# A trunk layer on one core: order of residual loads, of bank copies against weight casts, and start of the token sums

## The chip, the cores and the metric

The kernel runs on one core of one Trainium2 chip. The metric is the time of one execution in device microseconds (us); smaller is better. Times of before are the median of three runs; a run of the profiler adds one more execution whose instructions are known one by one.

## What is computed

One layer of a decoder, for 512 tokens and 1024 channels, all in float32. Cut to its steps:

```python
u = rmsnorm(h, norm1_g)
a_glu, q, k, v, r, g_low, gate_a, gate_b = split_cols(u @ w_in)
c = a_glu[..., :1024] * sigmoid(a_glu[..., 1024:])
y_conv = silu(layernorm(causal_dwconv(c, 31))) @ w_conv_out
y_gla = gated_linear_attention(q, k, v, g_low, r) @ w_gla_out
h = h + (sigmoid(gate_a) * y_conv + sigmoid(gate_b) * y_gla) @ w_o
u2 = rmsnorm(h, norm2_g)
z = causal_dwconv(u2 @ w_ffn_up, 3)                 # 2 x 2816 channels
h = h + (silu(z[..., :2816]) * z[..., 2816:]) @ w_ffn_down
return rmsnorm(h, final_g)
```

## The kernel before, in words

**Products.** A float32 operand is held as two parts, `hi` (its value rounded to float32r, the type in which TensorE takes it) and `lo` (what is left). One product of two operands is three matmuls (`mm3`, L363 to L365). A weight tile of 128x1024 is loaded into a buffer `raw` (four of them) by SP's queue, cast by ScalarE to `whi` (L295, L312), and its `wlo` is either subtracted by VectorE (L296, L321) or, for tiles in `ADDED`, made by a negating ScalarE copy (L314) and an accumulating load from GpSimd's queue (L315). `split_weight` does one tile, `prefetch(n)` as many as are missing until n tiles lie ready ahead of those used, and `weight` takes the next one, with `prefetch` around it. The order of all tiles is one list, `order`; asking for a tile out of this list's order isn't possible.

**Seven products for eight.** Some projections split rows and columns in halves and form a 2x2 block product with seven products instead of eight (`seven` for `w_o` and `w_down`, `unit` for `w_r`, `up_seven` for seven of the 22 pairs of the up projection, those in `UP_SEVEN`: 6, 7, 10, 11, 14, 15, 18). The steps are called a11, a12, s1, n2, n3, s4 and a22; sums of operands go into some of them. `up_seven(i)` uses four weights: b and x (two column tiles as loaded, x becoming a sum of both), n, and m (a half tile, cast at L288 and subtracted at L289 into a `raw` buffer). The sums of weights are `up_operand` (L257): two additions on VectorE, two on GpSimd, when x is asked for. While TensorE runs the steps, it also runs parts of another tile's product (`beside`) between them.

**Banks in `up_seven`.** One bank, `x` here (a PSUM bank, `ax` in the profile), takes a11, then n2 is added to it, then n3. In between ScalarE copies it out: after a11 into `n0` (L1456), after n2 negated into `n1` (L1462), after n3 into `n0` (L1466). The next step that writes to the bank has to wait for the copy. Bank `y` (s1) is copied into `att` at L1459. VectorE then makes two sums (L1468, L1469), and the convolution of width 3 (L1266 on ScalarE, L1268 on VectorE), Silu (L1274), the product of both halves (L1276) and the parts for the down projection (L1281 ScalarE's cast, L1282 and L1289 to L1301 VectorE) follow.

**Output projection.** `seven("w_o", ...)` adds its products into the residual, eight tiles `hres[t, n]` of 128x512, token tile t and column half n (L1188). The tiles are loaded from x at L1221, all from SP's queue, just ahead of it. Step a11 and a12 add to [0, 0] and [1, 0], s1 to [2, 1] and [3, 1], n2 and s4 to [0, 1] and [1, 1], n3 to [2, 1] and [3, 1], a22 to [2, 0] and [3, 0].

**Token sums.** The up projection by seven needs sums of the normed tokens (`up_sums`: `form` L1410 on VectorE, `place` L1419 and L1423 on ScalarE and VectorE). They stand in a list, `chains`, of pieces of work with a share each, and `fill(n)`, called at each weight, takes pieces until n shares are used up.

**What sets the order.** Each engine runs its instructions in the order of the program, and a waiting one holds up those behind it. A framework orders the instructions of an engine from the order in which the code issues them and a cost model's due times, sets the waits, and turns the buffers of a pool; so an edit can move instructions that it doesn't name.

Of the kernel before, what the change touches and what calls it, by code (L numbers as in the profile page):

```python
# [14 lines left out]
AF = mybir.ActivationFunctionType  # L15
# [5 lines left out]
NT = T // P  # L21
# [54 lines left out]
def trunk_layer(ctx: ExitStack, tc: tile.TileContext, a: dict, out: bass.AP):  # L76
    nc = tc.nc
# [31 lines left out]
    def nm(s):  # L109
        return f"{s}_{next(names)}"  # L110
# [16 lines left out]
    def mm_bank():  # L127
        return ps.tile([P, T], F32, tag="mm", name=nm("mm"), bufs=5)

    def ax_bank():  # L130
        return ps.tile([P, T], F32, tag="ax", name=nm("ax"), bufs=3)
# [193 lines left out]
    def prefetch(n):  # L325

        while len(ready) < min(used[0] + n, len(order)):
            split_weight()

    def weight(name, j, ahead=LOOK):  # L330
        assert order[used[0]] == (name, j)
        prefetch(1)
        used[0] += 1
        prefetch(ahead)
        fill(RATES.get(name, RATE))
        return ready[used[0] - 1]
# [6 lines left out]
    def fill(n):  # L343
        room[0] += n
        while chains and room[0] > 0:
            room[1] += 1
            chain = chains[room[1] % min(2, len(chains))]
            share, work = chain.pop(0)
            room[0] -= share
            with tc.issue_after(pace[0].ins):  # L350
                work()
            if not chain:
                chains.remove(chain)
                if not chains and after:
                    chains.append(after.pop()())
        if not chains:
            room[0] = 0.0

    def mm3(acc, l, r, first, last, more=False):

        (lh, ll), (rh, rl) = l, r
        kw = {"skip_group_check": True} if more else {}
        nc.tensor.matmul(acc, ll, rh, start=first, stop=False, **kw)  # L363
        nc.tensor.matmul(acc, lh, rl, start=False, stop=False, **kw)  # L364
        nc.tensor.matmul(acc, lh, rh, start=False, stop=last, **kw)  # L365
# [165 lines left out]
    def by_token(x):  # L531
        return x.rearrange("p (k t) -> p k t", t=P)
# [285 lines left out]
    for k in range(KT):  # L818
        s = slice(k * P, (k + 1) * P)
# [291 lines left out]
    H = T // 2  # L1111
# [103 lines left out]

    hres = {}
    ss2 = {}
    for t in range(NT):
        for n in range(2):
            hres[t, n] = rp.tile([P, T], F32, tag="hres", name=nm("hres"), bufs=2 * NT)  # L1220
            nc.sync.dma_start(hres[t, n], a["x"][t * P : (t + 1) * P, n * T : (n + 1) * T])  # L1221

# [161 lines left out]
    def up_sums():  # L1384

        def parts(name):
            if name == "n3":
                one = tp.tile([P, D], F32R, tag="gain", name=nm("n3h"), bufs=1)
                two = [tp.tile([P, T], F32R, tag="btmp", name=nm("n3l"), bufs=2) for _ in range(2)]
                return one, two  # L1390
            tags = {"s1": (tp, tp), "n2": (tp, fp), "s4": (fp, None)}[name]
            made = []
            for where in tags:
                if where is tp:
                    made.append(tp.tile([P, D], F32R, tag="x", name=nm(name), bufs=3))
                elif where is fp:
                    made.append(fp.tile([P, D], F32R, tag="u7", name=nm(name), bufs=2))
                else:
                    made.append([fp.tile([P, T], F32R, tag="u7s", name=nm(name), bufs=2) for _ in range(2)])
            return made  # L1400

        def form(name, i):
            q = lambda half, row: fu[2 * half + i, row]
            dst, x, y, op = {
                "s1": lambda: (q(1, 1), q(1, 0), q(1, 1), ALU.subtract),
                "n2": lambda: (q(1, 1), q(1, 1), q(0, 0), ALU.subtract),
                "s4": lambda: (q(0, 1), q(0, 1), q(1, 1), ALU.add),
                "n3": lambda: (q(1, 0), q(0, 0), q(1, 0), ALU.subtract),
            }[name]()
            nc.vector.tensor_tensor(dst, x, y, op)  # L1410

        def place(name, i):
            if name not in sums2:
                sums2[name] = parts(name)
            src = fu[{"s1": (2 + i, 1), "n2": (2 + i, 1), "s4": (i, 1), "n3": (2 + i, 0)}[name]]
            hi, lo = sums2[name]
            halves = [(0, 4)] if not isinstance(lo, list) else [(0, 2), (2, 4)]
            view = lambda x, k0, k1: x.rearrange("p (k t) -> p k t", t=H)[:, k0:k1, i * P : (i + 1) * P]
            nc.scalar.copy(view(hi, 0, 4), by_token(src))  # L1419
            for n, (k0, k1) in enumerate(halves):  # L1420
                dst = view(lo, 0, 4) if len(halves) == 1 else view(lo[n], 0, 2)
                high = view(hi, k0, k1).bitcast(F32)
                nc.vector.tensor_tensor(dst, by_token(src)[:, k0:k1, :], high, ALU.subtract)  # L1423

        chain = []
        for i in range(2):
            for name in ("s1", "n2", "s4"):
                chain += [(1, lambda name=name, i=i: form(name, i)), (1, lambda name=name, i=i: place(name, i))]
            chain.append((1, lambda i=i: form("n3", i)))
        return chain + [(1, lambda i=i: place("n3", i)) for i in range(2)]  # L1430

    def moving(step, k):
        if step in sums2:
            hi, lo = sums2[step]
            c = slice(k * H, (k + 1) * H)
            if isinstance(lo, list):
                return hi[:, c], lo[k // 2][:, (k % 2) * H : (k % 2 + 1) * H]
            return hi[:, c], lo[:, c]
        half, row = {"a11": (0, 0), "a12": (0, 1), "a22": (1, 1)}[step]
        return tuple(x[:, k, half * H : (half + 1) * H] for x in u2[row])  # L1440

    def up_seven(i, beside, done):

        n0, n1, bx, by = mm_bank(), mm_bank(), ax_bank(), ax_bank()
        x, y = bx[:, :H], by[:, :H]

        def step(name, acc, w, c, opens, more):
            for k in range(4):
                s = slice(c * T + k * P, c * T + (k + 1) * P)
                mm3(acc, (w[0][:, s], w[1][:, s]), moving(name, k), opens and k == 0, k == 3, not opens)  # L1450
            for _ in range(more):
                beside()

        wb, wx, wn, wm = (weight("w_up7", (i, s), 0) for s in "bxnm")
        step("a11", x, wb, 0, True, 1)
        nc.scalar.copy(n0[:, :H], x)  # L1456
        step("s1", y, wx, 0, True, 1)
        ys = att.rearrange("p a c -> p (a c)")[:, :H]
        nc.scalar.copy(ys, y)  # L1459
        step("n2", x, wx, 1, False, 1)  # L1460
        prefetch(1)
        nc.scalar.activation(n1[:, :H], x, AF.Copy, scale=-1.0)  # L1462
        step("a12", n0[:, :H], wb, 1, False, 2)
        prefetch(2)
        step("n3", x, wn, 0, False, 1)
        nc.scalar.copy(n0[:, H:], x)  # L1466
        step("s4", n1[:, :H], wn, 1, False, 2)
        nc.vector.tensor_tensor(n1[:, H:], ys, x, ALU.subtract)  # L1468
        nc.vector.tensor_tensor(n1[:, :H], ys, n1[:, :H], ALU.add)  # L1469
        done()  # L1470
        prefetch(3)
        step("a22", n0[:, H:], wm, 0, False, 0)
        prefetch(4)
        return n0, n1
# [9 lines left out]
    for gi, pairs in enumerate(GROUPS):  # L1484
# [17 lines left out]
        for p, q in pairs:  # L1502
            if q in UP_SEVEN:
                gate = col_tile(weight("w_up", p), acts2)
                products = by_parts(weight("w_up", FT + p))
                value, first = [], []
                beside = lambda: value.append(next(products))
                accs = up_seven(q, beside, lambda: first.append(first_of_pair(p, [gate, value[0]])))
                acts.append(second_of_pair(q, accs, *first[0]))
                continue  # L1510
            w, found = first_of_pair(p, both(p))
            acts.append(second_of_pair(q, both(q), w, found))
# [96 lines left out]
```

## Time and profile before

| what | us |
|---|---|
| median of three runs | 834.26 |
| lowest, highest run | 832.58, 834.54 |
| profiled execution, as timed | 834.23 |
| its span in the profile | 832.5 |
| TensorE busy | 820.5 |
| VectorE busy | 666.2 |
| ScalarE busy | 451.6 |
| GpSimd busy | 106.3 |

Rows of the profile name the start (from the start of the span), the duration, the engine (PE is TensorE's matmul, PEld its weight load, DVE VectorE, ACT ScalarE, POOL GpSimd, SP SyncE), the line, the operation, the tile written and the tiles read, and in brackets the idle time before and what ended it. A matmul's duration holds its way through the array, and several are under way at once; how fast they follow each other is seen from start to start. A line can be a helper's.

The output projection lies at about 440 to 480, the up and down projections from 480 on; blocks 6 and 7 of `up_seven` start at about 533 and 554, blocks 10, 11, 14, 15 and 18 end the list.

### The profile page before, as it was taken

To read this page: it belongs to the slowest core of one execution; us is meant where nothing else is said; L and a number is where in the kernel's file an instruction comes from. 1 tells how busy PE (TensorE), PEld (TensorE's weight loads), DVE (VectorE), ACT (ScalarE), POOL (GpSimd) and SP (SyncE) were. 2 spreads that over 40 slices of the span, in tenths; PEclk is the share of its full clock that TensorE was granted. 3 is DMA by queue.
4 is the path that set the end of the run, shared out by engine and by line. 5 is a ranking of instruction groups with operands and counts; after the bars stand their busy time and mean duration, and the time that the engine had idled before them with its cause. 6 is when DMAs were issued, how large, how long until landed. Compare 5 with 4: busy or idle time off the path is not lost.

```text
span 832.5 us, 10904 instructions
## 1 busy us (share of the span) xinstructions
PE 820.5 (99%) x4069; PEld 692.7 (83%) x4069; DVE 666.2 (80%) x985; ACT 451.6 (54%) x650; POOL 106.3 (13%) x127
## 2 busy tenths in 40 slices
PE   9999999999999999999999999999999999999996
PEld 7888887888888888888887898888788888988885
DVE  5999965989899991874787888679868788588896
ACT  6853437762633553158544668555446643667554
POOL 1000102000211221000001012111112011220011
PEclk9999999999999999999999999999999999999999
DMA  9875547722546578321446639256825637557562
GB/s 341 278 217 137 138 122 159 221 101 79 129 114 154 136 199 192 112 76 52 139 96 184 190 126 253 76 142 148 227 82 150 174 84 221 152 152 193 138 126 102
DMA packets 43973, 127.21 MB, mean 153 GB/s; under 512 B 4272, under 2 KB 12736, under 8 KB 43920
## 3 DMA queue, kind: packets, MB, share of 16 engines
q1 hardware_dynamic: 33232, 88.82, 30.3%
q0 software_dynamic: 10512, 37.49, 25.9%
q8 instruction: 32, 0.52, 0.3%
q14 instruction: 21, 0.17, 0.1%
q10 hardware_dynamic: 176, 0.20, 0.1%
HBM read 124.40 MB, written 6.29 MB: 157 GB/s over the span
## 4 chain that ended last, share of the span: by engine, by line
PE 66%; DVE 17%; DMA 7%; issue 4%; ACT 3%; POOL 2%; SPq 0%; POOLq 0%; ACTq 0%; DVEq 0%
PE mm L364 20%; PE mm L363 20%; PE mm L365 20%; DVE c L716 7%; DVE wlo L296 2%; PE ax L363 2%; PE ax L364 2%; PE ax L365 2%; DMA raw<-in_w_down_dram 2%; POOL rstd L411 1%; DMA kept<-rows 1%; DMA h<-in_x_dram 1%; PE mm L609 1%; DMA hres<-in_x_dram 1%; DVE hres L1188 1%
## 5 line engine op out<-in xcount | busy, mean ns | idle before, releaser
L363 PE MATMUL mm<-uh,wlo 128*128 128x512 f32 (+1 forms) x620 | 234.5, 378 | 0.0
L364 PE MATMUL mm<-ul,whi 128*128 128x512 f32 (+1 forms) x620 | 232.1, 374 | 0.6 <-DVE ul L454 0.6
L365 PE MATMUL mm<-uh,whi 128*128 128x512 f32 (+1 forms) x620 | 231.6, 374 | 0.0
L716 DVE SCALAR_TENSOR_TENSOR c<-h,pp,c 128x507 f32<-128x507 f32 (+21 forms) x240 | 162.4, 733 | 1.2 <-ACT c L713 0.6
L365 PEld LDWEIGHTS mm<-uh,whi 128*128 128x128 f32 x620 | 116.7, 188 | 21.1
L364 PEld LDWEIGHTS mm<-ul,whi 128*128 128x128 f32 x620 | 116.9, 189 | 20.0 <-DVE ul L454 1.1
L363 PEld LDWEIGHTS mm<-uh,wlo 128*128 128x128 f32 x620 | 116.9, 188 | 19.1 <-issue 0.2
L312 ACT CAST whi<-raw 128x1024 fp32r<-128x1024 f32 x94 | 97.5, 1043 | 53.3 <-PE mm L365 43.2
L314 ACT ACTIVATE wlo<-raw 128x1024 fp32r<-128x1024 f32 x41 | 43.5, 1060 | 75.9 <-PE mm L363 68.7
L295 ACT CAST whi<-raw 128x1024 fp32r<-128x1024 f32 (+1 forms) x51 | 51.7, 1024 | 44.7 <-PE mm L365 31.9
L1268 DVE SCALAR_TENSOR_TENSOR tmp<-mm,pp,tmp 128x511 f32<-128x511 f32 x88 | 64.9, 744 | 10.6 <-ACT tmp L1266 10.0
L321 DVE TENSOR_TENSOR wlo<-raw,whi 128x1024 fp32r<-128x1024 f32 x53 | 64.3, 1221 | 11.0 <-ACT whi L312 10.2
L296 DVE TENSOR_TENSOR wlo<-raw,whi 128x1024 fp32r<-128x1024 f32 (+1 forms) x51 | 62.9, 1243 | 9.2 <-ACT whi L295 8.6
L295 ACT CAST whi<-kept 128x1024 fp32r<-128x1024 f32 (+1 forms) x40 | 40.0, 1005 | 38.0 <-PE mm L365 16.7
L296 DVE TENSOR_TENSOR wlo<-kept,whi 128x1024 fp32r<-128x1024 f32 (+1 forms) x40 | 46.5, 1168 | 14.8 <-ACT whi L295 14.7
L1266 ACT ACTIVATE tmp<-mm,pp 128x512 f32<-128x512 f32 x44 | 33.3, 774 | 12.0 <-PE mm L365 12.0
L1188 DVE TENSOR_TENSOR hres<-hres,mm 128x512 f32<-128x512 f32 (+1 forms) x49 | 32.4, 670 | 5.5 <-DMA hres<-in_x_dram 3.9
L315 POOL DMA_DIRECT2D wlo<-in_w_up_dram x18 | 15.6, 864 | 98.0 <-ACT wlo L314 87.5
L364 PE MATMUL mm<-wlo,sh 128*128 128x512 f32 x66 | 25.9, 393 | 0.0
L365 PE MATMUL mm<-whi,sh 128*128 128x512 f32 x66 | 25.7, 389 | 0.0
L363 PE MATMUL mm<-whi,sl 128*128 128x512 f32 x66 | 25.2, 391 | 0.2 <-ACT whi L295 0.2
L364 PE MATMUL mm<-h,whi 128*128 128x512 f32 x64 | 25.0, 391 | 0.1
(357 smaller groups left out, 1630.4 us busy)
## 6 DMA issues: line engine op xcount, KB each, us to landing
raw<-in_w_up_dram SPq DMA_DIRECT2D x44, 512.0 KB, 4.9
wlo<-in_w_up_dram POOLq DMA_DIRECT2D x18, 512.0 KB, 7.4
raw<-in_w_glu_dram SPq DMA_DIRECT2D x16, 512.0 KB, 6.4
raw<-in_w_down_dram SPq DMA_DIRECT2D x15, 512.0 KB, 5.2
kept<-in_w_down_dram POOLq DMA_DIRECT2D x10, 512.0 KB, 5.4
raw<-in_w_v_dram SPq DMA_DIRECT2D x8, 512.0 KB, 5.6
rows<-in_w_r_dram SPq DMA_DIRECT2D x16, 256.0 KB, 6.6
raw<-in_w_qk_dram SPq DMA_DIRECT2D x8, 512.0 KB, 3.2
```

Of the source, the lines that this page charges most:

```text
L295: nc.scalar.copy(hi, raw)
L296: pace[0] = nc.vector.tensor_tensor(lo, raw, hi.bitcast(F32), ALU.subtract)
L312: nc.scalar.copy(hi, raw)
L314: nc.scalar.activation(lo, raw, AF.Copy, scale=-1.0)
L321: pace[0] = nc.vector.tensor_tensor(lo, raw, hi.bitcast(F32), ALU.subtract)
L363: nc.tensor.matmul(acc, ll, rh, start=first, stop=False, **kw)
L364: nc.tensor.matmul(acc, lh, rl, start=False, stop=False, **kw)
L365: nc.tensor.matmul(acc, lh, rh, start=False, stop=last, **kw)
L716: nc.vector.scalar_tensor_tensor(y[:, s:], c[:, : T - s], w, y[:, s:], ALU.mult, ALU.add)
L1188: nc.vector.tensor_tensor(hres[t, n][:, c], hres[t, n][:, c], x[:, c], op)
L1266: nc.scalar.activation(z, acc, AF.Identity, bias=pp[:, PP_FB + m : PP_FB + m + 1], scale=w[2])
L1268: nc.vector.scalar_tensor_tensor(z[:, s:], acc[:, : T - s], w[j], z[:, s:], ALU.mult, ALU.add)
```

## The change

The residual tiles are issued in another order; in `up_seven` the weights n and m are taken after n2's copy instead of at the start, the calls to `prefetch(1)` and `prefetch(2)` move behind copies, and the chain of token sums starts with an entry that does nothing and takes three shares.

```diff
     hres = {}
     ss2 = {}
-    for t in range(NT):
-        for n in range(2):
+    for n, ts in ((0, (0, 1)), (1, (2, 3)), (1, (0, 1)), (0, (2, 3))):
+        for t in ts:
             hres[t, n] = rp.tile([P, T], F32, tag="hres", name=nm("hres"), bufs=2 * NT)
             nc.sync.dma_start(hres[t, n], a["x"][t * P : (t + 1) * P, n * T : (n + 1) * T])
...
-        chain = []
+        chain = [(3, lambda: None)]
         for i in range(2):
             for name in ("s1", "n2", "s4"):
...
-        wb, wx, wn, wm = (weight("w_up7", (i, s), 0) for s in "bxnm")
+        wb, wx = (weight("w_up7", (i, s), 0) for s in "bx")
         step("a11", x, wb, 0, True, 1)
         nc.scalar.copy(n0[:, :H], x)
         step("s1", y, wx, 0, True, 1)
         ys = att.rearrange("p a c -> p (a c)")[:, :H]
         nc.scalar.copy(ys, y)
         step("n2", x, wx, 1, False, 1)
+        nc.scalar.activation(n1[:, :H], x, AF.Copy, scale=-1.0)
+        wn, wm = (weight("w_up7", (i, s), 0) for s in "nm")
         prefetch(1)
-        nc.scalar.activation(n1[:, :H], x, AF.Copy, scale=-1.0)
         step("a12", n0[:, :H], wb, 1, False, 2)
-        prefetch(2)
         step("n3", x, wn, 0, False, 1)
         nc.scalar.copy(n0[:, H:], x)
+        prefetch(2)
         step("s4", n1[:, :H], wn, 1, False, 2)
```

## Prediction

> **What bounds the kernel now.** I read the page first, then the waits of TensorE, then the timeline around each of those waits, engine by engine.
>
> ```profile
> span 832.5 us, 10904 instructions
> ```
> ```profile
> PE 820.5 (99%) x4069; PEld 692.7 (83%) x4069; DVE 666.2 (80%) x985; ACT 451.6 (54%) x650; POOL 106.3 (13%) x127
> ```
> TensorE bounds it: it holds the span almost without a gap, so a change that leaves its matmuls alone can only win back single stalls. The changed program has the same matmuls in the same order. The profiled execution took 834.23 us, that is 1.7 beside the span, and the median of the runs is 834.26, so sums against the one hold for the other.
>
> ```profile
> PE ax L364 <- DVE wlo L296: 1.1, 1, 1.1
> ```
> ```profile
> PE ax L363 <- ACT mm L1462: 0.5, 1, 0.5
> PE ax L363 <- ACT mm L1456: 0.3, 1, 0.3
> ```
> ```profile
> PEld ax L363 <- ACT mm L1462: 1.9, 4, 0.9
> ```
> Columns: total us, times, longest. Matmuls are pipelined, so these waits understate the loss; I measure it from start to start. Three of the waits lie where the diff works: one in the output projection, two kinds in the up projection by seven products. The last row, of weight loads, says that the second kind comes four times.
>
> **Residual tiles.** Rows of TensorE, of VectorE and of the loads:
>
> ```profile
> 448.95 0.39 PE L365 MATMUL mm<-whi,sums 128*128 128x512 f32 x1
> 449.18 0.39 PE L363 MATMUL ax<-whi,h 128*128 128x512 f32 x1
> 450.62 0.50 PE L364 MATMUL ax<-wlo,h 128*128 128x512 f32 x1 [1.05 <-DVE wlo L296]
> 450.96 0.40 PE L365 MATMUL ax<-whi,h 128*128 128x512 f32 x1
> ```
> ```profile
> 443.51 0.68 DVE L1129 TENSOR_TENSOR sums<-tmp,sums 128x512 fp32r<-128x512 f32 x1
> 448.14 0.69 DVE L1188 TENSOR_TENSOR hres<-hres,mm 128x512 f32<-128x512 f32 x1 [3.94 <-DMA hres<-in_x_dram]
> 448.75 0.69 DVE L1129 TENSOR_TENSOR sums<-tmp,sums 128x512 fp32r<-128x512 f32 x1
> 449.35 1.22 DVE L296 TENSOR_TENSOR wlo<-raw,whi 128x1024 fp32r<-128x1024 f32 x1
> ```
> ```profile
> DMA to landing us min/median/max: 2.5/8.4/8.8
> ```
> ```profile
> DMA to landing us min/median/max: 4.8/4.8/4.8
> ```
> A matmul of 512 columns starts 0.23 after the one before (448.95 to 449.18). The step to 450.62 takes 1.44 and the next 0.34: lost are 1.21 + 0.11 = 1.32 us. The cause stands on VectorE: its second addition wants tile [1, 0], third in the queue, and sits idle for 3.94 us; the split of a weight, which has nothing to do with it, waits behind in order and ends at 450.57, while TensorE wanted it at 449.41.
>
> After the change [1, 0] is second of the same eight loads. The first of the two landing rows is for all eight, from issue to landing; the second is the answer of the same view for the stretch that holds the second issue, at 438.9: it landed 4.8 later, at 443.7. VectorE is free at 443.51 + 0.68 = 444.19, so the addition starts at 444.2, the split ends near 446.6, 2.8 us before TensorE asks, and all 1.32 go. Eight loads are issued from the same places of SP's queue, so nothing behind them moves. a11, a12 and s1 read the four tiles that now come first; of those that fall back, [0, 1] and [1, 1] are read by n2 and [2, 0] and [3, 0] by a22, the last step, and the slowest of the eight took 8.8. Bounds: nothing, if the second place landed as late as the third did, to 1.32. I take 1.3.
>
> **Copies ahead of casts.** In a block of seven, n2 adds into the bank that a11 filled, and n3 into it again; each must wait until ScalarE has copied the bank out (L1456, then L1462). Three stretches of TensorE, n2 and n3 of block 7 and n3 of block 11:
>
> ```profile
> 557.76 0.39 PE L365 MATMUL mm<-uh,whi 128*128 128x512 f32 x1
> 558.45 0.38 PE L363 MATMUL ax<-n,wlo 128*128 128x256 f32 x1 [0.30 <-ACT mm L1456]
> 558.67 0.28 PE L364 MATMUL ax<-n,whi 128*128 128x256 f32 x1
> 558.78 0.28 PE L365 MATMUL ax<-n,whi 128*128 128x256 f32 x1
> ```
> ```profile
> 563.26 0.39 PE L365 MATMUL mm<-uh,whi 128*128 128x512 f32 x1
> 564.11 0.39 PE L363 MATMUL ax<-n3h,wlo 128*128 128x256 f32 x1 [0.46 <-ACT mm L1462]
> 564.33 0.28 PE L364 MATMUL ax<-n3l,whi 128*128 128x256 f32 x1
> ```
> ```profile
> 644.85 0.39 PE L365 MATMUL mm<-uh,whi 128*128 128x512 f32 x1
> 645.14 0.39 PE L363 MATMUL ax<-n3h,wlo 128*128 128x256 f32 x1
> 645.37 0.28 PE L364 MATMUL ax<-n3l,whi 128*128 128x256 f32 x1
> ```
> A step of 256 columns takes 0.11 to 0.12 (558.67 to 558.78). So n2 of block 7 loses 0.46 + 0.11 = 0.57, its n3 0.62 + 0.10 = 0.72, and n3 of block 11 0.06 + 0.11 = 0.17. The four weight-load waits above are those of blocks 7, 11, 15 and 18; the last two I price as block 11: 3 x 0.17 = 0.5.
>
> ```profile
> 556.03 0.63 ACT L1274 ACTIVATE tmp<-tmp 128x512 f32<-128x512 f32 x1 [1.96 <-DVE tmp L1268]
> 556.57 0.60 ACT L1281 CAST yh<-w 128x512 fp32r<-128x512 f32 x1
> 557.08 1.05 ACT L295 CAST whi<-raw 128x1024 fp32r<-128x1024 f32 x1
> 558.03 0.36 ACT L1456 COPY mm<-ax 128x256 f32<-128x256 f32 x1
> ```
> ```profile
> 562.95 0.83 ACT L1281 CAST sh<-v 128x768 fp32r<-128x768 f32 x1 [0.81 <-DVE v L1301]
> 563.69 0.37 ACT L1462 ACTIVATE mm<-ax 128x256 f32<-128x256 f32 x1
> ```
> The order of the built program says what moves. In all seven blocks the negating copy goes ahead of one or two casts; in blocks 7, 11, 15, 18 also ahead of the cast of `sh` (0.83, after a wait of 0.81 for VectorE). It then follows the end of n2 by at most one cast, some 3 us before n3. So 0.72 + 0.5 go whole: 1.2, bounds 0.7 (if a cast still stands in front in 11, 15, 18) to 1.2.
>
> L1456 is different: in block 7 it still has the cast of the n weight and the Silu in front; the order there changes by what VectorE does before. To find where it lands I walk block 7 in before's times.
>
> ```profile
> 541.91 4.78 DMA raw<-in_w_up_dram
> ```
> ```profile
> L257 DVE TENSOR_TENSOR raw<-raw,raw x14: 679/689/1782, 519.4 to 745.9; 128x512 f32<-128x512 f32 x14
> ```
> ```profile
> 547.71 1.73 DVE L257 TENSOR_TENSOR raw<-raw,raw 128x512 f32<-128x512 f32 x1
> ...
> 551.49 1.88 DVE L296 TENSOR_TENSOR wlo<-raw,whi 128x1024 fp32r<-128x1024 f32 x1
> ```
> ```profile
> 547.60 1.29 POOL L257 TENSOR_TENSOR raw<-raw 128x512 f32<-128x512 f32 x1 [3.28 <-DVE raw L257]
> ```
> ```profile
> 555.86 0.28 PE L363 MATMUL ax<-s,wlo 128*128 128x256 f32 x1
> ```
> Block 6 now casts its m weight one cast (1.05) later, 0.95 less the overlap of neighbours; m's buffer takes block 7's x weight, so that load is issued at 542.86 and, at 4.78, lands at 547.64. VectorE's second sum (547.71) took 1.73 against a median of 0.689, for GpSimd's addition ran beside it to 548.89; the sum ended 0.55 after it, at 549.44. The split at 551.49 took 1.88 against 1.22 in the same way. So I put such operations behind each other: first sum to 548.4, split 1.22, GpSimd's addition 1.29, and the second sum ends 0.55 later, 551.4 at the latest. The cast of the sum follows to 552.4, three vector steps (0.74, 0.74, 0.68) run beside it to 553.3, and its split, now alone, takes 1.22 to 554.4; before it ended at 553.37. Behind it: `w` 554.8, ScalarE's m copy 555.0, `yh` 555.5, the n cast 556.5, Silu 557.05, L1456 557.4. TensorE asks at 557.99 (557.76 + 0.23) and had to wait until 558.39 before: the wait goes, with 0.6 to spare. The load may take longer, since its neighbours, two accumulating loads of GpSimd, now start closer to it. I take 0.45 of 0.57; bounds nothing to 0.57.
>
> [...]
>
> **Token sums.** The entry without work at the head of the chain takes three shares, so fewer sums are issued at the first weight. In the built program the sums stand in the same places of VectorE's, ScalarE's and GpSimd's orders as before. Cost and gain nothing; if they did move, they would run beside matmuls of weights that are ready.
>
> **Sum.** 1.3 + 1.2 + 0.45 = 2.95; off that 0.1 for block 18, for which the m cast of block 15 moves back further and the x weight's landing comes near its use: 2.85. 834.23 - 2.85 = **831.4 us**, 0.34% faster. I call 0.3% (2.5 us) about what a measurement of this kernel can tell from no change.
>
> **Rivals.**
> 1. *One part does not pay*: either the second residual tile lands as late as the third did (all eight share the engines with an accumulating load), which takes 1.3, or block 7 keeps its waits, which takes 0.72 + 0.45. Result 832.6 to 832.7. For it: the landings jump from 4.8 to over 8. Against: the second place has a landing in the trace.
> 2. *The x weight of the next block is late (slower).* Its load now starts 0.95 us later in blocks 7, 11 and 15, about 1.5 in 18, next to two accumulating loads. The split that s1 reads would come at 554.4, TensorE asks at 555.86: 1.5 us of cover. If the load takes 8.8 instead of 4.78, as the slowest residual tile did, each of the four blocks stalls 2.5 us: -2.95 + 10 = 7 slower, 841. It decides from a load of 6.3; even at 7.1 it only eats the gain (4 x 0.8 = 3.2, 834.5). Against: the same load beside the same neighbours took 4.78.
> 3. *The stalls come back later*: VectorE is 80% busy, and if it sets the pace behind block 7, a TensorE 2 us ahead meets it there. Result 833 to 834.2. Against: VectorE's queue is released there by TensorE's own banks and moves with it.
>
> **How the numbers follow.** Forecast (all parts pay, 830.2 to 832.0) 0.55; rival 1 0.2; rival 3 0.13; rival 2 0.12, of it 0.06 at 834 to 836.7 and 0.06 above. The range 830.0 to 834.3 leaves out about 0.1 above and less below. Faster by over 0.3% means below 831.7: most of the forecast's case and nothing else, 0.52. Within 0.3%: the rest of it, rivals 1 and 3, half of 2, 0.42. Slower: 0.06.
>
> **What would show it.** In the profile after: VectorE's second addition of the residual without its 3.94 of idle time and no 1.44 step of TensorE there (residual order); no weight-load wait for L1462's copy, and n2 of block 7 within 0.3 of the matmul before it (copies). Wrong it would be by a wait of s1's first matmul in blocks 7, 11, 15 or 18 for a split, or by larger steps of TensorE after 570 than before.

## The result, and the profile after

The changed kernel takes 837.48 us (median; 835.70 to 838.13) beside 833.98 for the kernel before: ratio 1.0039, 95% interval [1.0029, 1.0050], so 3.3 us slower [2.4, 4.2]. The profiled execution took 837.71, its span 836.0, 3.5 above that of before.

The page after, and its waits of TensorE (total us, times, longest), answer to the rows shown of before:

```profile
span 836.0 us, 10899 instructions
PE 821.5 (98%) x4069; PEld 692.1 (83%) x4069; DVE 665.9 (80%) x985; ACT 450.8 (54%) x650; POOL 107.0 (13%) x127
```
```profile
PE ax L363 <- DVE wlo L296: 2.3, 4, 1.1
...
PE mm L363 <- DMA wlo<-in_w_up_dram: 0.9, 2, 0.5
PE ax L363 <- ACT mm L1456: 0.6, 1, 0.6
...
PE mm L363 <- DVE yl L1282: 0.3, 1, 0.3
```
Of the three waits that the change was to take away two are gone from this list: that of the output projection for a split and those for the copy of L1462 (now L1461). The third, for the copy of L1456, is there still, 0.6 instead of 0.3. New are a wait that comes four times, for a split (`wlo`, L296), two for accumulating loads and one for `yl`. The timeline of TensorE at the places quoted of before, in the output projection and in block 7:

```profile
449.48 0.39 PE L363 MATMUL ax<-whi,h 128*128 128x512 f32 x1
449.71 0.39 PE L364 MATMUL ax<-wlo,h 128*128 128x512 f32 x1
...
554.48 0.39 PE L365 MATMUL mm<-uh,whi 128*128 128x512 f32 x1
555.33 0.38 PE L363 MATMUL ax<-s,wlo 128*128 128x256 f32 x1 [0.46 <-DVE wlo L296]
555.55 0.28 PE L364 MATMUL ax<-s,whi 128*128 128x256 f32 x1
...
557.33 0.39 PE L365 MATMUL mm<-uh,whi 128*128 128x512 f32 x1
558.30 0.39 PE L363 MATMUL ax<-n,wlo 128*128 128x256 f32 x1 [0.58 <-ACT mm L1456]
...
563.13 0.39 PE L365 MATMUL mm<-uh,whi 128*128 128x512 f32 x1
563.36 0.28 PE L363 MATMUL ax<-n3h,wlo 128*128 128x256 f32 x1
```
The step of 1.44 in the output projection is 0.23. n3 of block 7 starts at once, where it lost 0.72. But s1 starts 0.85 after the matmul ahead of it: 0.62 lost, and 0.10 in its next step. n2 loses 0.74 + 0.11, more than the 0.57 of before.

Where the 3.5 us came from, by matching TensorE's 4069 matmuls, whose order is the same in both: start of the kernel +0.3; output projection -1.4; block 7 +0.3 (s1 +0.7, n2 +0.3, n3 -0.7); `yl` at 576 +0.6; block 11 +1.3; an accumulating load that is late at 658 +0.8; block 15 +0.7; block 18 +0.5; another late one at 774 +0.7; small drifts, -0.3, make up the rest.

The cause of the first new wait is read from three engines. ScalarE, before:

```profile
538.36 1.06 ACT L314 ACTIVATE wlo<-raw 128x1024 fp32r<-128x1024 f32 x1
539.33 1.03 ACT L312 CAST whi<-raw 128x1024 fp32r<-128x1024 f32 x1
540.26 0.36 ACT L1462 ACTIVATE mm<-ax 128x256 f32<-128x256 f32 x1
540.56 0.60 ACT L288 CAST wm<-raw 128x512 fp32r<-128x512 f32 x1
541.07 1.05 ACT L312 CAST whi<-raw 128x1024 fp32r<-128x1024 f32 x1
542.02 1.05 ACT L314 ACTIVATE wlo<-raw 128x1024 fp32r<-128x1024 f32 x1
```
and after:

```profile
537.21 1.06 ACT L314 ACTIVATE wlo<-raw 128x1024 fp32r<-128x1024 f32 x1
538.17 0.37 ACT L1461 ACTIVATE mm<-ax 128x256 f32<-128x256 f32 x1
538.48 1.03 ACT L312 CAST whi<-raw 128x1024 fp32r<-128x1024 f32 x1
539.41 1.05 ACT L314 ACTIVATE wlo<-raw 128x1024 fp32r<-128x1024 f32 x1
540.37 0.60 ACT L288 CAST wm<-raw 128x512 fp32r<-128x512 f32 x1
```
The copy (L1462, L1461) goes ahead of a cast, as meant. The m cast (L288) falls behind the cast, and also behind the second negating copy of a weight (L314), which it was ahead of before. Each L314 releases an accumulating load of GpSimd; the m cast, with its subtraction, releases the buffer for block 7's x weight. GpSimd's loads, before, then after:

```profile
539.83 0.87 POOL L315 DMA_DIRECT2D wlo<-in_w_up_dram  x1 [11.74 <-ACT wlo L314]
543.48 0.84 POOL L315 DMA_DIRECT2D wlo<-in_w_up_dram  x1 [2.78 <-ACT wlo L314]
```
```profile
538.67 0.87 POOL L315 DMA_DIRECT2D wlo<-in_w_up_dram  x1 [11.76 <-ACT mm L1461]
540.87 0.85 POOL L315 DMA_DIRECT2D wlo<-in_w_up_dram  x1 [1.32 <-ACT wlo L314]
```
Block 7's x weight was issued at 541.91 between the two; now it is issued behind both. The chain of waits after gives that load in block 7 and in block 11, and the view of GpSimd's second load in block 6 how long that took to land:

```profile
541.72 6.88 DMA raw<-in_w_up_dram
...
624.75 8.27 DMA raw<-in_w_up_dram
```
```profile
DMA to landing us min/median/max: 7.6/7.6/7.6
```
6.88 instead of 4.78. It lands at 548.60; the accumulating load ahead of it at 540.87 + 7.56 = 548.43.

### The profile page after: what moved, and what is told of

Same layout as the page of the kernel before. It is cut to its first block, busy times and chain, and to the rows that moved or that the text cites. A ratio compares the mean times of both kernels' runs of the same rounds, so it can differ in the third digit from the quotient of the medians.

```text
span 836.0 us, 10899 instructions
## 1 busy us (share of the span) xinstructions
PE 821.5 (98%) x4069; PEld 692.1 (83%) x4069; DVE 665.9 (80%) x985; ACT 450.8 (54%) x650; POOL 107.0 (13%) x127
## 4 chain that ended last, share of the span: by engine, by line
PE 72%; issue 9%; DMA 7%; DVE 7%; ACT 4%; POOL 1%; POOLq 0%; SPq 0%; ACTq 0%; DVEq 0%
PE mm L363 21%; PE mm L364 21%; PE mm L365 21%; DMA raw<-in_w_up_dram 3%; DMA wlo<-in_w_up_dram 2%; PE ax L363 2%; PE ax L365 1%; PE ax L364 1%; DVE tmp L1268 1%; PE mm L609 1%; DVE raw L257 1%; PE ax L1027 1%; ACT whi L312 1%; DVE wlo L296 1%; DMA x<-in_x_dram 1%
## 5 line engine op out<-in xcount | busy, mean ns | idle before, releaser
L314 ACT ACTIVATE wlo<-raw 128x1024 fp32r<-128x1024 f32 x41 | 43.4, 1059 | 76.0 <-PE mm L363 68.8
L295 ACT CAST whi<-raw 128x1024 fp32r<-128x1024 f32 (+1 forms) x51 | 51.7, 1024 | 52.1 <-PE mm L365 33.5
L296 DVE TENSOR_TENSOR wlo<-raw,whi 128x1024 fp32r<-128x1024 f32 (+1 forms) x51 | 62.3, 1231 | 10.9 <-ACT whi L295 10.4
L296 DVE TENSOR_TENSOR wlo<-kept,whi 128x1024 fp32r<-128x1024 f32 (+1 forms) x40 | 46.6, 1169 | 14.8 <-ACT whi L295 14.6
```

Source lines behind the costliest of these rows:

```text
L295: nc.scalar.copy(hi, raw)
L296: pace[0] = nc.vector.tensor_tensor(lo, raw, hi.bitcast(F32), ALU.subtract)
L314: nc.scalar.activation(lo, raw, AF.Copy, scale=-1.0)
```

## Experiments

Ratios are to runs of the kernel before on the same chip, and a difference is the ratio's share of their time. e9 leaves out half of a weight's correction, so it is a measurement and no candidate.

| kernel | median us | ratio, 95% interval | difference us |
|---|---|---|---|
| changed kernel | 837.48 | 1.0039 [1.0029, 1.0050] | +3.3 |
| e1: residual order | 833.70 | 0.9997 [0.9987, 1.0008] | -0.3 |
| e2: copy's line | 838.11 | 1.0052 [1.0035, 1.0070] | +4.3 |
| e3: e2, second accumulating load gated | 835.81 | 1.0021 [1.0010, 1.0032] | +1.8 |
| e4: e2, m cast held ahead | 833.32 | 0.9994 [0.9983, 1.0005] | -0.5 |
| e5: the rest of the change | 833.43 | 1.0007 [0.9998, 1.0016] | +0.6 |
| e6: e4 and residual order | 832.52 | 0.9994 [0.9984, 1.0005] | -0.5 |
| e7: e3 without a new tile | 831.10 | 0.9975 [0.9963, 0.9986] | -2.1 |
| e8: e7 and residual order | 832.10 | 0.9989 [0.9980, 0.9998] | -0.9 |
| e9: e2, second accumulating load halved | 831.72 | 0.9972 [0.9956, 0.9987] | -2.3 |
| e10: before, tiles 128 bytes on | 838.82 | 1.0052 [1.0037, 1.0067] | +4.3 |
| e11: before, tiles 1024 bytes on | 833.61 | 0.9995 [0.9984, 1.0006] | -0.4 |

The theory: the x weight's load is long because the second accumulating load was issued ahead of it and shares the DMA engines with it. Rivals: the load's later issue alone; the residual order, which brings TensorE earlier; the rest of the change.

### Which part carries the loss: e1, e2, e5

```diff
-    for t in range(NT):
-        for n in range(2):
+    for n, ts in ((0, (0, 1)), (1, (2, 3)), (1, (0, 1)), (0, (2, 3))):
+        for t in ts:
```


> Only the order of the eight residual tiles is changed. Theory (the loss of the whole change comes from the copy's line alone): VectorE's second residual addition no longer waits, the 1.44 us step of TensorE near 450.6 goes, nothing else moves: 1.3 us less, about 832.6. Rival (the loss comes from the residual order, which lets TensorE arrive in the blocks of seven earlier): stalls of s1's first matmul show up here, about 836 or more.

No loss, and a gain below what the runs can tell: -0.3 [-1.1, +0.7]. Neither figure of the two theories came. The stall of before's profile is why: see e5.

```diff
         step("n2", x, wx, 1, False, 1)
-        prefetch(1)
         nc.scalar.activation(n1[:, :H], x, AF.Copy, scale=-1.0)
+        prefetch(1)
         step("a12", n0[:, :H], wb, 1, False, 2)
```


> Only the line of the first negating copy is moved ahead of the prefetch. Theory: it carries the whole loss. The x weights of blocks 7 and 11 take 6.9 and 8.3 us to land again (4.8 and 5.6 before), s1's first matmul waits for the split in blocks 7, 11, 15 and 18, the waits for L1462's copy are gone; without the residual order's 1.3 us the time is about 4.8 us above before, 838.8. Rival (the loss needs both parts, because only a TensorE that is 1.3 us ahead meets the late split): 2 us above before or less, 836 at most.

This one line carries the whole loss, +4.3 [2.9, 5.8], without the residual order. Its waits of TensorE:

```profile
PE mm L363 <- DMA wlo<-in_w_up_dram: 2.5, 2, 1.9
PE ax L363 <- DVE wlo L296: 2.0, 4, 0.5
```
VectorE's first sum in block 7 starts when the x weight, issued at 543.10, has landed:

```profile
550.05 0.69 DVE L257 TENSOR_TENSOR raw<-raw,raw 128x512 f32<-128x512 f32 x1 [3.23 <-DMA raw<-in_w_up_dram]
```
The load took 6.93 again (7.67 in blocks 11 and 15).

```diff
-        chain = []
+        chain = [(3, lambda: None)]
...
-        wb, wx, wn, wm = (weight("w_up7", (i, s), 0) for s in "bxnm")
+        wb, wx = (weight("w_up7", (i, s), 0) for s in "bx")
...
+        wn, wm = (weight("w_up7", (i, s), 0) for s in "nm")
         prefetch(1)
         nc.scalar.activation(n1[:, :H], x, AF.Copy, scale=-1.0)
         step("a12", n0[:, :H], wb, 1, False, 2)
-        prefetch(2)
         step("n3", x, wn, 0, False, 1)
         nc.scalar.copy(n0[:, H:], x)
+        prefetch(2)
```


> The rest of the change (token sums that begin later, n and m weights asked for later, the second prefetch moved), without the copy's line and without the residual order. Theory: each engine carries out the same order as before, so nothing changes, 0 within 1 us, the waits for L1462's copy stand at 1.9 us in weight loads, and the step near 450.6 is 1.44 in some executions and not in others, since the third residual tile's landing hangs on whether it is issued ahead of GpSimd's accumulating load. Rival (this rest carries a part of the loss): 1 us or more above before.

+0.6 [-0.2, +1.3]: no loss that can be told from none. It has the old residual order and the same order of instructions as before, and yet no stall near 450.6. GpSimd's accumulating load of `w_o` beside the residual tiles, in before's profile and in e5's, and VectorE's second residual addition in e5:

```profile
439.53 0.88 POOL L242 DMA_DIRECT2D raw<-in_w_o_dram  x1 [8.10 <-DVE h L1119]
```
```profile
440.98 0.89 POOL L242 DMA_DIRECT2D raw<-in_w_o_dram  x1 [9.12 <-DVE h L1120]
```
```profile
444.53 0.68 DVE L1188 TENSOR_TENSOR hres<-hres,mm 128x512 f32<-128x512 f32 x1
```
In before's profile the third residual tile was issued at 439.70, behind GpSimd's load, and took 8.34. In e5 it was issued at 439.76, ahead of it, and took 4.06. The order of these two issues does not decide alone. Nine profiles have the old order. In three (e4, e5, e7) the tile went ahead of GpSimd's load and took 4.1 to 4.8; in four (before, e3, e9, e10) it went about 0.2 behind and took 7.9 to 8.3; in e2 and e11 it went 0.2 behind too and took only 5.0 and 5.2. What else it takes stays open. The stall stands in the four (1.32 in before's, 0.59 in e3, 0.74 in e9, 0.78 in e10) and in no profile with the new order. The mean of the nine is 0.4 us, so that is about what the residual order can win on average; e1's interval holds it. Not all of it arrives: in e1's profile the step is gone, but n2 of block 7, where TensorE now comes earlier, loses 1.12 instead of before's 0.57.

### Late issue or neighbour: e4, e3, e7

```diff
...
+                    m_cast[:] = [nc.scalar.copy(both[:, :T], raw), 0]
...
+                with ExitStack() as behind_m:
+                    if m_cast:
+                        m_cast[1] += 1
+                        if m_cast[1] == 2:
+                            behind_m.enter_context(tc.issue_after(m_cast[0].ins))
                     nc.scalar.activation(lo, raw, AF.Copy, scale=-1.0)
                     nc.gpsimd.dma_start(lo, a[name][spec], accum_op=ALU.add)
...
```


> As e2, but in the blocks before the x loads of blocks 7, 11 and 15 the second negating copy of the weight halves, and the accumulating load behind it, stand behind the m cast again, as before the change. Theory: the x load is issued at its old time and takes 4.8 to 5.6 us, s1 does not wait in blocks 7, 11 and 15, the gain of L1462's copy (about 1.2 us) is left: 832.8. Both theory and the rival of the later issue give this; a third, that the moved copy itself makes ScalarE late for s1, gives s1's waits again, 837 or more.

-0.5 [-1.4, +0.4]. With the m cast ahead of the second negating copy again, the loads take 4.90 and 5.38 in blocks 7 and 11, and s1 waits nowhere, so the moved copy itself harms nothing. In its profile n3's waits are gone, but n2 of block 7 loses 0.3 more than in before's and `yl` 0.5, so less than 1.2 is left. Ahead of L1456 ScalarE has before's order there, the Silu first and the n cast last, so that n2 is not relieved; why `yl` waits stays open.

```diff
...
                 nc.scalar.activation(lo, raw, AF.Copy, scale=-1.0)
+                if m_split:
+                    m_split[1] += 1
+                    if m_split[1] == 2:
+                        seen = small(1, "seen")
+                        gated = nc.gpsimd.tensor_copy(seen, m_split[0][:, T : T + 1].bitcast(F32))
+                        with tc.issue_after(gated.ins):
+                            nc.gpsimd.dma_start(lo, a[name][spec], accum_op=ALU.add)
...
```


> As e2, but GpSimd reads a column of the m weight's split ahead of the second accumulating load, so this load cannot be issued before the x weight's load; the m cast still comes one cast later than before. Theory (the x load is long because the second accumulating load was issued ahead of it): it takes 4.8 to 5.6 us again, s1's waits go or shrink below 0.3 us each, the time is between 832.8 and 834.5. Rival (the later issue of the x load alone makes s1 wait): s1's waits stay at 0.5 to 1.3 us in four blocks, 837 or more.

+1.8 [0.8, 2.7], between the two. Its profile has no wait of s1, n2 or n3 in any block of seven, as the theory has it, but between 3 and 4 us more in steps of TensorE that are about 2% longer. The clock granted there was 1.00 (windows 404:436 and 782:822), as in before's, so it is not what made them longer. That was new; e7 takes out what could have caused it.

```diff
-                        seen = small(1, "seen")
+                        seen = small(NT, "mean")[:, :1]
```


> As e3, but the column that GpSimd reads goes into a tile that is there already, so no other tile is placed elsewhere in SBUF. In e3's profile s1, n2 and n3 had no waits at all in the blocks of seven, yet in long stretches without waits (304 to 350, 396 to 440, 780 to 821) each step of TensorE was 2% longer, about 3 us in all. Theory (the new tile's place in SBUF made the steps longer, and the contention was cured): steps of 226.7 ns as before, waits gone as in e3, 832.0 to 833.0. Rival (the steps belong to the gate or to chance): 835 or more, or again long steps.

-2.1 [-3.1, -1.2]: the fastest kernel here that computes the whole layer. Its x weight for block 7, by SP, and GpSimd's column and second accumulating load; then VectorE's first sum; then TensorE at s1:

```profile
541.79 0.33 SPq L201 DMA_DIRECT2D raw<-in_w_up_dram  x1
```
```profile
541.83 0.18 POOL L321 COPY mean<-wm 128x1 f32<-128x1 f32 x1 [2.22 <-DVE wm L290]
542.45 0.85 POOL L323 DMA_DIRECT2D wlo<-in_w_up_dram  x1 [0.44 <-ACT whi L314]
```
```profile
545.44 0.69 DVE L258 TENSOR_TENSOR raw<-raw,raw 128x512 f32<-128x512 f32 x1
```
```profile
554.54 0.39 PE L377 MATMUL mm<-uh,whi 128*128 128x512 f32 x1
554.77 0.28 PE L375 MATMUL ax<-s,wlo 128*128 128x256 f32 x1
```
The load is issued no earlier than in the changed kernel (541.72), but ahead of the second accumulating load. It takes 3.63 (3.87 and 3.67 in blocks 11 and 15), and s1 starts 0.23 after the matmul ahead of it. The rival of late issue falls for blocks 7, 11 and 15.

### Order or bytes: e9

```diff
...
-                nc.gpsimd.dma_start(lo, a[name][spec], accum_op=ALU.add)
+                m_split[:] = [n + 1 for n in m_split]
+                part = slice(0, T) if m_split == [2] else slice(0, D)
+                nc.gpsimd.dma_start(lo[:, part], a[name][spec][:, part], accum_op=ALU.add)
...
```


> As e2, but the second accumulating load, which is issued ahead of the x weight's, brings only the first half of its columns (the other half of that weight's correction is left out). Order and places of issue are e2's. Theory (the x weight waits behind the bytes that are ahead of it on the DMA engines): its loads of blocks 7, 11 and 15 fall from 6.9, 7.7 and 7.7 us to about 5 to 6, s1's waits for the split go, and the time falls by 3 us or more against e2, to 833 to 835. Rival (the order of issue or GpSimd's queue makes them long, not the bytes): loads and s1's waits as in e2, about 838.

-2.3 [-3.7, -1.1]. The orders are those of e2; only bytes are fewer, for half of a weight's correction is left out. SP's x load, GpSimd's load ahead of it, and the first sum that waits for the landing:

```profile
544.22 0.33 SPq L201 DMA_DIRECT2D raw<-in_w_up_dram  x1
```
```profile
543.37 0.85 POOL L319 DMA_DIRECT2D wlo<-in_w_up_dram  x1 [1.33 <-ACT wlo L316]
```
```profile
549.42 0.69 DVE L258 TENSOR_TENSOR raw<-raw,raw 128x512 f32<-128x512 f32 x1 [1.48 <-DMA raw<-in_w_up_dram]
```
5.18 (5.93 and 5.08 in blocks 11 and 15) against e2's 6.93, 7.67 and 7.67, and the waits for s1, n2, n3 and late accumulating loads are gone, as in e7; only `yl` still loses 0.4. So it is the bytes of the second accumulating load, with the order as it was.

### Versions with both parts: e6, e8

Both add e1's edit, e6 to e4 and e8 to e7.

> The residual order together with e4's copy order. Theory: the gains of both stand beside each other: e4's profile lost 1.3 us less than before at L1462's waits and 0.9 more elsewhere, and the residual order takes the 450.6 step out of those executions that have it: 0.5 to 1.5 us below before, about 832.8. Rival (a TensorE that comes 1.3 us earlier meets the x weight in the blocks of seven): no gain or a loss against e4.

> e7 with the residual order. Theory: 0.5 to 1.3 us below e7, 831 to 832.5, the best of all. Rival: the s1 waits come back because TensorE is earlier by the residual step: no better than e7.

e6 is -0.5 [-1.3, +0.4], e8 -0.9 [-1.7, -0.2]. Neither beats the version without the residual order; by e5's count there were 0.4 us to win, less than these runs can tell. No s1 wait came back in either profile, so the rival falls too. Why e8's median lies above e7's, where its span is 0.2 shorter, stays open.

### Where operands lie: e10, e11

```diff
+    nc.gpsimd.memset(small(1, "seen"), 0.0)
```


> The kernel before with one small unused tile of 128 bytes a partition ahead of the others, so that the operand tiles lie 128 bytes further on, as in e3. Theory (the place of TensorE's operands in SBUF lengthened e3's steps): stretches with steps near 231 ns instead of 226.7, 2 to 4 us more, 836. Rival (it was chance): 0.

```diff
+    nc.gpsimd.memset(small(64, "seen"), 0.0)
```


> The same with a tile of 1024 bytes, so that the operand tiles keep their places to a multiple of 1024 bytes. Theory: no longer steps, 0 within 1 us. Rival (any other place costs, or chance): as e10.

+4.3 [3.1, 5.6] and -0.4 [-1.3, +0.5]. The timeline of TensorE in e10, first and last of eight matmuls that follow each other, and of eight in before's at the same time:

```profile
409.80 0.39 PE L367 MATMUL mm<-ch,whi 128*128 128x512 f32 x1
...
411.43 0.40 PE L365 MATMUL mm<-ch,wlo 128*128 128x512 f32 x1
```
```profile
409.74 0.39 PE L363 MATMUL mm<-ch,wlo 128*128 128x512 f32 x1
...
411.33 0.39 PE L364 MATMUL mm<-c,whi 128*128 128x512 f32 x1
```
Seven steps in 1.63 against 1.59: 233 ns each instead of 227, with no wait. With a shift of 1024 bytes the step is 227 again. Both kernels carry the same added instruction, so it is the size of the tile that counts. So e3's long steps came from the new tile's place, and e7 against e3 (-2.1 and +1.8) shows what that cost there.

## Why the prediction was wrong, point by point

The forecast was 831.4 us; the changed kernel took 837.48.

**Residual tiles, 1.3: the mechanism was right, the size held for one execution only.** In the profile after, VectorE's second addition waits for nothing and the step is gone, as written. But the stall is an accident of some executions (e5), and the term is worth at most about 0.4 on average. The bounds "nothing to 1.32" held; the value was taken at the upper end because a single profile was read as every run.

**Copies, n3, 1.2: right.** All four waits are gone in the changed kernel. e7 shows the term by itself: 0.73 in block 7 and 0.17 to 0.19 in blocks 11, 15 and 18.

**Copies, n2 of block 7, 0.45: the step that failed.** It is the sentence "that load is issued at 542.86 and, at 4.78, lands at 547.64". TensorE runs 1.15 ahead of before at that place (555.33 - 0.62 = 554.71 against 555.86); put into before's times, the load was issued at 541.72 + 1.15 = 542.87, as walked, and landed at 549.75: 2.1 later than walked, all of it in the load. The walk behind the landing held. VectorE after, first sum and the split that s1 reads:

```profile
548.63 0.69 DVE L257 TENSOR_TENSOR raw<-raw,raw 128x512 f32<-128x512 f32 x1 [3.18 <-DMA raw<-in_w_up_dram]
...
554.06 1.21 DVE L296 TENSOR_TENSOR wlo<-raw,whi 128x1024 fp32r<-128x1024 f32 x1
```
That the 1.73 and the 1.88 of the walk come with GpSimd's addition beside them was the author's estimate from before's rows, and what holds the two up no run shows. After, that addition ran from 549.46 to 551.60, the second sum ended at 552.15, again 0.55 behind it, and the split, with no addition beside it, took 1.21. From landing to the end of that split it is 6.67, walked were 6.76. So the cover of 1.5 was right, the load overran it by 0.6, and s1 lost 0.62 and 0.10 in its next step. The prediction had noted that the load may take longer, and took off 0.12 for it here (0.45 of 0.57) and 0.1 for block 18. Instead of 0.45 won, n2 lost 0.85 in place of 0.57. With the same order and a short load (e7) n2's wait went whole, 0.57, and with n3's the copies gained 1.85 from block 7 on, against 1.65 predicted. The 0.57 is itself the figure of one execution: e1, e5, e10 and e11, which have before's order of copies, lose 1.12, 1.01, 1.10 and 0.87 there.

**Rival 2** named the late load, and its sign, a wait of s1 for a split in blocks 7, 11, 15 and 18, is what the profile shows. It named the point too: "It decides from a load of 6.3". The load was 6.88, 8.27 and 7.61 in blocks 7, 11 and 15. What spoke against it, "the same load beside the same neighbours took 4.78", was false in one word: the neighbours were the same, but one of them had moved ahead of it. The walk had followed one cast (the m cast, one place back) and not the second negating copy that passed it, nor the accumulating load which that copy releases. The rival's price was also short. s1 lost 0.72 + 1.38 + 0.72 + 0.56 = 3.4 in the four blocks, near the 3.2 given for a load of 7.1; n2 lost 0.7 more in the four blocks, and two accumulating loads were late by 1.4 together, which the rival did not have. Both are gone in e7 and e9 with the late load. The 0.6 of `yl` are not its doing: `yl` waits in e4 and e9 too, where s1 does not.

**Block 18** has a load of only 4.82, but issued at 744.11 against 738.67, of which 2.5 are TensorE's own delay. The prediction had 1.5 for the rest and it was 2.9. In e7 and e9, which have e2's order of copies without the late splits, this load is issued 11.6 ahead of s1 and s1 does not wait; in the changed kernel and in e2 it is issued 10.4 ahead of the place where s1 would have started. So 1.2 of the 2.9 came with the late loads of the blocks ahead; by which instruction is not shown.

**Token sums, 0: right** within e5's interval. **Rival 1** came true twice: for the residual tiles on average, for another reason than given, and for n2 of block 7. **Rival 3** did not come about behind block 7: in e7 TensorE leaves the last block with a lead of 2.9 us over before's profile and keeps it to the end.

## What to carry to other kernels

When an instruction moves ahead, list what it passes, and for each passed instruction the transfer that it releases: a load's duration from the trace holds only for the loads that were under way beside it then (block 7's x weight: 4.78 before, 6.88 after). Before a stall of one profile is priced, take a second profile, and look whether its cause hangs on two issues a few tenths of a us apart; it is worth its share of the executions. And where a gain is eaten, keep it and gate the neighbour: one column read by GpSimd turned e2's 4.3 us of loss into e7's 2.1 of gain.

## What the runs showed of the hardware

**Loads of two queues shared the DMA engines, 79 packets of the one beside 79 of the other.** The same 128x1024 tile took 3.2 with no other load under way (529.88 to 533.08 after), 4.8 to 5.6 where one accumulating load was issued ahead of it (before), and 6.9 to 8.3 where two were. With two, SP's x load landed 0.17, 0.16 and 0.20 us after GpSimd's second accumulating load in blocks 7, 11 and 15 of the changed kernel, and 0.24, 0.19 and 0.21 after it in e9, where that load was half as large. The packets show how they shared. Between 544.5 and 547 of the changed kernel, block 7's x weight is on SP's queue (q1) and the second accumulating load on GpSimd's (q0); the columns are packets, MB, and the share of 16 engines' time:

```profile
q0 software_dynamic: 79, 0.32, 65.8%
q1 hardware_dynamic: 79, 0.32, 34.3%
```
There are as many packets of the one as of the other, 4 KB each. By its share, a packet of the accumulating load held an engine for 0.658 * 16 * 2.5 / 79 = 0.33 us, one of the x weight for 0.17. So for each packet of the x weight the engines carried one of the other load, which took twice as long. The same in e9, between 546.8 and 548:

```profile
q0 software_dynamic: 62, 0.12, 54.8%
q1 hardware_dynamic: 60, 0.25, 53.8%
```
There a packet of the accumulating load is half as large and took 0.17 us. In the changed kernel the x weight's packets begin at 543.8, where those of the first accumulating load end and those of the second begin. The two loads landed 0.16 to 0.24 us apart, whether the packets of one were whole or half, and beside the half ones block 7's x weight took 5.18 instead of e2's 6.93. In what order an engine took the packets of the two queues is not shown; these are counts over a stretch. Why block 11's load took 1.4 us more than block 7's is not separated.

**A small tile added ahead of the others lengthened TensorE's step.** With one of 128 bytes: 233 ns instead of 227 in the stretch shown, 4.3 us in all; with one of 1024 bytes: nothing (e10, e11). Other stretches keep their step: between 40 and 120 us it is 226.7 ns in both kernels and in before's. Which of the moved tiles does it, and from which distance on, no run shows. In e3, too, it was one new small tile.

**The clock fell after a gap of 2.3 us.** In e2's profile TensorE started no matmul between 775.29 and 777.63, for it waited for an accumulating load. Windows of 2 us there, with TensorE's busy time and in the column after POOL's the granted clock:

```profile
776.00:778.00 2.00, 0.37 (x1) 0.31 (x2) 2.00 (x4) 1.90 (x3) 0.00 (x0) 0.97 1.03 404
778.00:780.00 2.00, 2.00 (x6) 1.57 (x5) 2.00 (x3) 0.94 (x2) 0.00 (x0) 0.50 0.95 381
```
In the next window, from 780, it is 0.68. So the clock was 0.50 in one window and below 1.00 in those beside it; estimated from these three figures, that cost 0.06 + 1.0 + 0.64 = 1.7 beside the stall's 2.1. The gap was 2.3 from start to start, 1.95 of them idle. Two shorter ones left the clock at 1.00: 1.12 idle before 639.01 in the profile after (windows 638:640 and 640:642), and 1.05 before 450.62 in before's (449:451 and 451:453). From what gap on it falls, no run shows. That execution is 4.3 above e2's median; whether the other long ones of e2 had the same is not shown.
